# Eight stationary operands of the weight matmuls moved to byte offsets that are no multiples of 32

## The chip, the cores and the metric

The kernel runs on one core of one Trainium2 chip. The metric is the device time of one execution in microseconds; less is better. Before the change, three runs took 1162.81, 1162.16 and 1159.4 us (median 1162.16 us). TensorE (PE in the profile) multiplies; its weight loads, which put the stationary operand into the array, have rows of their own (PEld). VectorE is DVE, ScalarE is ACT, GpSimd is POOL, and SP only issues DMAs.

## The reference, cut to what matters

One layer of a hybrid encoder on 256 tokens of width 2048:

```python
h = rms_norm(x, norm_g)
proj = h @ w_in                      # 2048 x 16512, split into 15 parts
ya = chunked_band_attention(...) * silu(az)
yb = rwkv7_time_mix(...) * silu(bz)
yc = memory_cross_attention(cq, mk, mv) * silu(cz)   # mk, mv from rms_norm(mem) @ w_mem_kv
merged = (sigmoid(ga) * (ya @ w_up_a) + sigmoid(gb) * (yb @ w_up_b)
          + sigmoid(gc) * (yc @ w_up_c))
return x + merged @ w_o
```

All tensors are float32. The weights (w_in, w_mem_kv, the three w_up and w_o) are read once each.

## The kernel before

**Matmuls with weights.** A float32 product is made of three matmuls in a faster float32 format (float32r): both sides are split into a high and a low part, and high*high, low*high and high*low are summed in PSUM. The weights come as one stream: a DMA on the SP queue brings 128 x 2048 numbers (1 MB) into a buffer `raw` (two buffers), and `wchunk` makes of each two halves `whi` (ACT, line 191) and `wlo` (DVE, line 193), in four buffers each. `proj` (lines 197 to 218) runs, for every 128 rows of the weights and each of the two halves of the tokens, the matmuls of lines 210, 211 and 215: the weights (`whi`, `wlo`) are the moving operand, 512 columns wide, and a 128 x 128 block of the activations is the stationary one:

```python
T.matmul(acc[tt], xh[:, kt + k2, sl], hv[:, k2], start=(kt + k2 == 0), stop=False)
T.matmul(acc[tt], xl[:, kt + k2, sl], hv[:, k2], start=False, stop=False)
```

So each of these matmuls has a weight load of its own, of 128 numbers (512 bytes) per partition. `proj_last` (lines 220 to 249) does the same for the last quarter of w_o, partly with 256 columns. `proj_cm` (lines 251 to 265) has the roles turned: a weight block is stationary, `xh` and `xl` move with 256 columns.

**The activations.** Each is held as a pair of tiles, high and low, of 128 partitions by k times 256 numbers. `xh`, `xl` hold the normalised x (k = 16) and are used all along. `mh`, `ml` (k = 16) hold the memory, and are written by `split_kt` (lines 309, 310) in the first 27 us. `ych`, `ycl` hold the cross-attention's output, `yah`, `yal` the band attention's; both pairs use the same two slots `yth`, `ytl` (k = 8) and are written by `split_y` (lines 373, 374). `yh`, `yl` (k = 8) hold the output of the time mixing, and `gh`, `gl` (k = 16) the merged result; `to_T` writes them (lines 389, 390).

**Where the tiles stand.** SBUF is a byte range per partition. The pools hand out places one after the other, from the left or (side="right") from the right, each tile rounded up to 32 bytes. Tiles that nothing uses (`padw`, 24 numbers; `padr`, 56 numbers) shift what stands behind them. By the built program's own addresses, every operand of lines 210 to 262 begins at a multiple of 64 bytes before the change. `padr` is the rightmost tile, then come `ytl`, `yth`, and left of them the right-hand pools that follow each other in time: `mkv` with `catt`, later `rwkv`.

**Order.** Instructions of an engine run in the order of the program. Small generators (`spawn`, `tick`, `finish`) weave the attention's and the time mixing's steps between the weight chunks. The change touches none of this.

Of the kernel before, what the change touches and what calls it, by code (L numbers as in the profile page):

```python
# [9 lines left out]
F32R = mybir.dt.float32r  # L10
# [7 lines left out]
S = 256  # L18
P = 128
# [71 lines left out]
def build(nc, tc, A, out, dbg=None):  # L91
    dbg = dbg or {}
    ctx = ExitStack()
    with ctx:
        _build(ctx, nc, tc, A, out, dbg)


def _build(ctx, nc, tc, A, out, dbg):
    uid = [0]

    def nm(s):
        uid[0] += 1
        return f"{s}_{uid[0]}"

    def pool(st, name, bufs=1, side=None, space=None):
        kw = {}
        if side:
            kw["side"] = side
        if space is not None:
            kw["space"] = space  # L110
        return st.enter_context(tc.tile_pool(name=name, bufs=bufs, **kw))

    V, SC, G, T = nc.vector, nc.scalar, nc.gpsimd, nc.tensor

    cp = pool(ctx, "const")
    wp = pool(ctx, "wts")
# [5 lines left out]
    def t(pl, shape, tag, dtype=F32, bufs=1):  # L122
        return pl.tile(shape, dtype, name=nm(tag), tag=tag, bufs=bufs)
# [19 lines left out]
    def spawn(gen, wait=0):  # L143
        tasks.append([wait, gen])
        tick(0)
        return gen
# [13 lines left out]
    def finish(gen):  # L160
        for tk in list(tasks):
            if tk[1] is gen:
                while tk in tasks:
                    advance(tk)
# [5 lines left out]
    def wload():  # L170
        i = wstate[0]
        wstate[0] += 1
        raw = t(wp, [P, 2048], "raw", bufs=2)
        if i == 0:
            for a, b in ((0, 512), (512, 1024), (1024, 2048)):
                nc.sync.dma_start(raw[:, a:b], A["wstream"][i][:, a:b])
                yield raw
        else:
            nc.sync.dma_start(raw, A["wstream"][i])
        while True:  # L180
            yield raw
# [198 lines left out]
    def to_T(src, yh, yl, k0, k1):  # L380
        for k in range(k0, k1, 4):
            banks = [psum([P, 2, S]) for _ in range(2)]
            for kk in range(4):
                for tt in range(2):
                    T.transpose(banks[kk // 2][:, kk % 2, tt * P:tt * P + P],
                                src[:, tt, (k + kk) * P:(k + kk + 1) * P], ident)
            for i, bank in enumerate(banks):
                ks = slice(k + 2 * i, k + 2 * i + 2)
                SC.copy(yh[:, ks, :], bank)
                V.tensor_tensor(out=yl[:, ks, :], in0=bank, in1=yh[:, ks, :].bitcast(F32), op=ALU.subtract)  # L390
            yield 1
# [5 lines left out]
    xl = t(xpool, [P, 16, S], "xl", F32R)  # L397

    padp = pool(ctx, "padr", side="right")
    t(padp, [P, 56], "padr")  # L400
    yc_st = ExitStack()
    ycp = pool(yc_st, "yc", side="right")
    ych = t(ycp, [P, 8, S], "yth", F32R)
    ycl = t(ycp, [P, 8, S], "ytl", F32R)

    cst_ = ExitStack()
    mkp = pool(cst_, "mkv", side="right")
# [1 line left out]
    mv = t(mkp, [P, 2, 1024], "mv")  # L409
    m_st = ExitStack()  # L410
    mp = pool(m_st, "memT")
    mh = t(mp, [P, 16, S], "mh", F32R)
    ml = t(mp, [P, 16, S], "ml", F32R)
    wld = wload()
    raw0 = next(wld)
    xr0 = t(mp, [P, 4, S], "xraw", bufs=2)
# [522 lines left out]
    dump("merged_c", merged)  # L939


    yah = t(ycp, [P, 8, S], "yth", F32R)
    yal = t(ycp, [P, 8, S], "ytl", F32R)
    at_st = ExitStack()
    ap_ = pool(at_st, "aatt")

# [96 lines left out]
    dump("y_b", zb)  # L1043
    g_st = ExitStack()
    gp = pool(g_st, "gb")
    yh = t(gp, [P, 8, S], "yh", F32R)
    yl = t(gp, [P, 8, S], "yl", F32R)
    yt = spawn(to_T(zb, yh, yl, 0, 8), 1)
    sigs.append(gate_sig(proj(xh, xl, 16), zbp, 8))
    finish(yt)  # L1050
    gh = t(gp, [P, 16, S], "gh", F32R)
    gl = t(gp, [P, 16, S], "gl", F32R)
    for j in range(4):
        up(yh, yl, j, False, sigs[j])
        mt = spawn(to_T(merged, gh, gl, j * 4, j * 4 + 4), 1)
# [79 lines left out]
```

## Time and profile before

| what | value |
|---|---|
| runs, median (lowest, highest) | 1162.16 us (1159.4, 1162.81) |
| the profiled execution | 1159.04 us |
| its span, first to last instruction | 1157.0 us |
| PE busy | 1141.6 us, 6650 records |
| PE weight loads busy | 966.9 us |
| DVE, ACT, POOL busy | 791.2, 521.9, 178.3 us |
| mean granted TensorE clock | 0.997 |

A PE record's length is not its cost, since matmuls overlap in the array: the cost is the distance from one start to the next. A float32r matmul has one record, a plain float32 one has two. The chain of waits follows the work that ended last back from the end; its pieces show how long a row of equal matmuls took.

### The profile page before, as it was taken

Reading aid. Unit: us, or ns where it says so; the run is one execution under the profiler, and the core shown is the slowest. Engines: PE = TensorE matmul, PEld = TensorE weight load, DVE = VectorE, ACT = ScalarE, POOL = GpSimd, SP = SyncE. Lnnn points to the kernel's source line nnn. Section 1 sums busy time; section 2 is a strip of 40 time slices with the busy share of each in tenths; the row PEclk is TensorE's granted clock in tenths of the full one; section 3 lists DMA queues with packets and bytes.
Section 4 is the critical chain, followed back from the end, with each engine's and each line's share of the span. In section 5 each row is a group of like instructions: output and inputs, shape, how many; then the busy total and the mean of one; then the engine's idle time right before and its main releaser. Section 6 shows DMA issues by size and latency. Waiting matters only on the chain.

```text
span 1157.0 us, 16950 instructions
## 1 busy us (share of the span) xinstructions
PE 1141.6 (99%) x6650; PEld 966.9 (84%) x6650; DVE 791.2 (68%) x1370; ACT 521.9 (45%) x647; POOL 178.3 (15%) x240
## 2 busy tenths in 40 slices
PE   8999999999999999999999989999999999999998
PEld 6888989889889778988997869887888877888887
DVE  6974556557769667879866678946687856557443
ACT  7754545443643434344633526442453343444431
POOL 0110000034110204010203310203301203300000
PEclk9999999999999999999999989999999999999999
DMA  8756535466464653565644445564355664654663
GB/s 272 263 205 204 191 134 182 155 201 209 163 234 150 205 188 142 186 210 164 201 147 146 139 164 176 165 206 148 127 205 183 201 218 146 203 195 156 234 231 109
DMA packets 36906, 212.75 MB, mean 184 GB/s; under 512 B 5087, under 2 KB 7391, under 8 KB 13275
## 3 DMA queue, kind: packets, MB, share of 16 engines
q1 hardware_dynamic: 29664, 198.59, 50.0%
q0 software_dynamic: 3936, 9.44, 3.1%
q10 hardware_dynamic: 3226, 3.65, 1.0%
q8 instruction: 52, 0.85, 0.3%
q14 instruction: 28, 0.22, 0.1%
HBM read 206.95 MB, written 3.67 MB: 182 GB/s over the span
## 4 chain that ended last, share of the span: by engine, by line
PE 82%; DVE 8%; DMA 5%; ACT 2%; issue 1%; POOL 1%; SPq 0%; ACTq 0%; DVEq 0%; POOLq 0%
PE pp L210 21%; PE pp L211 20%; PE pp L215 19%; PE pp L259 4%; PE pp L260 4%; DMA raw<-in_wstream_dram 4%; PE pp L262 4%; DVE wlo L193 3%; ACT whi L191 1%; DVE Xu L751 1%; DVE tmu L749 1%; PE pp L232 1%; PE pp L234 1%; PE pp L231 1%; PE ps L496 1%
## 5 line engine op out<-in xcount | busy, mean ns | idle before, releaser
L193 DVE TENSOR_TENSOR wlo<-raw,whi 128x1024 fp32r<-128x1024 f32 x368 | 455.3, 1247 | 264.2 <-ACT whi L191 258.1
L191 ACT CAST whi<-raw 128x1024 fp32r<-128x1024 f32 x368 | 381.5, 1051 | 559.6 <-PE pp L211 274.8
L210 PE MATMUL pp<-whi,xh 128*128 128x512 f32 x768 | 308.1, 401 | 0.7 <-ACT whi L191 0.6
L211 PE MATMUL pp<-whi,xl 128*128 128x512 f32 x768 | 300.5, 391 | 0.0
L215 PE MATMUL pp<-wlo,xh 128*128 128x512 f32 x768 | 205.9, 390 | 2.3 <-DVE wlo L193 2.3
L210 PEld LDWEIGHTS pp<-whi,xh 128*128 128x128 f32 x768 | 144.7, 188 | 33.5 <-ACT whi L191 1.2
L215 PEld LDWEIGHTS pp<-wlo,xh 128*128 128x128 f32 x768 | 144.3, 188 | 33.5 <-DVE wlo L193 3.2
L211 PEld LDWEIGHTS pp<-whi,xl 128*128 128x128 f32 x768 | 144.9, 189 | 28.3
L259 PE MATMUL pp<-xh,whi 128*128 128x256 f32 x528 | 131.7, 287 | 0.0
L260 PE MATMUL pp<-xl,whi 128*128 128x256 f32 x528 | 129.3, 283 | 0.0
L259 PEld LDWEIGHTS pp<-xh,whi 128*128 128x128 f32 x528 | 101.0, 191 | 1.1 <-issue 0.3
L260 PEld LDWEIGHTS pp<-xl,whi 128*128 128x128 f32 x528 | 101.1, 192 | 0.4
L262 PE MATMUL pp<-xh,wlo 128*128 128x256 f32 x528 | 74.1, 283 | 0.0
L262 PEld LDWEIGHTS pp<-xh,wlo 128*128 128x128 f32 x528 | 68.1, 192 | 0.0
L210 PE MATMUL pp<-whi,mh 128*128 128x512 f32 x128 | 51.5, 402 | 2.7 <-ACT whi L191 2.3
L210 PE MATMUL pp<-whi,yth 128*128 128x512 f32 x128 | 51.1, 399 | 0.0
L211 PE MATMUL pp<-whi,ml 128*128 128x512 f32 x128 | 50.5, 394 | 0.0
L211 PE MATMUL pp<-whi,ytl 128*128 128x512 f32 x128 | 49.9, 390 | 0.0
L749 DVE TENSOR_TENSOR tmu<-Tu,Xu 128x112 f32<-128x112 f32 (+29 forms) x124 | 32.7, 263 | 9.5 <-DMA Tu<-scrt 6.3
L210 PE MATMUL pp<-whi,gh 128*128 128x512 f32 x96 | 37.4, 390 | 0.0
L211 PE MATMUL pp<-whi,gl 128*128 128x512 f32 x96 | 37.4, 389 | 0.0
L879 POOL TENSOR_TENSOR s0z<-st,fx 64x128 f32<-64x128 f32 x24 | 11.0, 458 | 168.2 <-DVE st L873 124.9
(258 smaller groups left out, 1367.1 us busy)
## 6 DMA issues: line engine op xcount, KB each, us to landing
raw<-in_wstream_dram SPq DMA_DIRECT2D x184, 1024.0 KB, 4.9
xraw<-in_xT_dram SPq DMA_DIRECT2D x8, 256.0 KB, 4.5
Tu<-scrt POOLq DMA_DIRECT2D x4, 512.0 KB, 4.1
xr<-in_x_dram POOLq DMA_DIRECT2D x8, 256.0 KB, 4.6
xraw<-in_memT_dram SPq DMA_DIRECT2D x7, 256.0 KB, 4.8
out_dram<-xr POOLq DMA_DIRECT2D x6, 256.0 KB, 3.8
bias<-in_rel_dram POOLq DMA_DIRECT2D x4, 256.0 KB, 4.1
tmpA<-in_bc_dram ACTq DMA_DIRECT2D x8, 128.0 KB, 4.1
```

Source lines behind the costliest of these rows:

```text
L191: SC.copy(hi, sl)
L193: V.tensor_tensor(out=lo, in0=sl, in1=hi.bitcast(F32), op=ALU.subtract)
L210: T.matmul(acc[tt], xh[:, kt + k2, sl], hv[:, k2], start=(kt + k2 == 0), stop=False)
L211: T.matmul(acc[tt], xl[:, kt + k2, sl], hv[:, k2], start=False, stop=False)
L215: T.matmul(acc[tt], xh[:, kt + k2, sl], lv[:, k2], start=False, stop=(last and k2 == 1))
L231: T.matmul(acc, xh[:, kt + k2, sl], hv[:, k2, cs], start=(kt + k2 == 0), stop=False)
L232: T.matmul(acc, xl[:, kt + k2, sl], hv[:, k2, cs], start=False, stop=False)
L234: T.matmul(acc, xh[:, kt + k2, sl], lv[:, k2, cs], start=False, stop=(kt + k2 == nk - 1))
L259: T.matmul(acc, hv[:, k2], xh[:, kt + k2, :], start=(kt + k2 == 0), stop=False)
L260: T.matmul(acc, hv[:, k2], xl[:, kt + k2, :], start=False, stop=False)
L262: T.matmul(acc, lv[:, k2], xh[:, kt + k2, :], start=False, stop=(kt + k2 == 15))
L749: V.tensor_tensor(out=tv, in0=Tu[:, s, s + 1:32].unsqueeze(2).to_broadcast([P, n, m]), in1=X[:, s:s + 1, 0:m].to_broadcast([P, n, m]), op= ...
```

## The change

`toff` makes a tile that is 8 numbers (32 bytes) per partition larger and returns a slice of it that begins `off` numbers in. The eight tiles are made by it, the offsets being 2, 4 or 6 numbers, so 8, 16 or 24 bytes. `padr` shrinks from 56 to 48 numbers, and a new unused tile `pady` (56 numbers) stands at the head of the pool of `yh`, `yl`, `gh`, `gl`.

```diff
+    def toff(pl, k, tag, off):
+        v = t(pl, [P, k * S + 8], tag, F32R)
+        return v[:, off:off + k * S].rearrange("p (k s) -> p k s", s=S)
...
-    t(padp, [P, 56], "padr")
+    t(padp, [P, 48], "padr")
...
-    ych = t(ycp, [P, 8, S], "yth", F32R)
-    ycl = t(ycp, [P, 8, S], "ytl", F32R)
+    ych = toff(ycp, 8, "yth", 2)
+    ycl = toff(ycp, 8, "ytl", 2)
...
-    mh = t(mp, [P, 16, S], "mh", F32R)
-    ml = t(mp, [P, 16, S], "ml", F32R)
+    mh = toff(mp, 16, "mh", 4)
+    ml = toff(mp, 16, "ml", 4)
...
-    yah = t(ycp, [P, 8, S], "yth", F32R)
-    yal = t(ycp, [P, 8, S], "ytl", F32R)
+    yah = toff(ycp, 8, "yth", 2)
+    yal = toff(ycp, 8, "ytl", 2)
...
-    yh = t(gp, [P, 8, S], "yh", F32R)
-    yl = t(gp, [P, 8, S], "yl", F32R)
+    t(gp, [P, 56], "pady")
+    yh = toff(gp, 8, "yh", 4)
+    yl = toff(gp, 8, "yl", 6)
...
-    gh = t(gp, [P, 16, S], "gh", F32R)
-    gl = t(gp, [P, 16, S], "gl", F32R)
+    gh = toff(gp, 16, "gh", 6)
+    gl = toff(gp, 16, "gl", 4)
```

The places that follow, in bytes within a partition, by the addresses of the two built programs:

| operand | begins before | begins after | rest by 32 | rest by 64 |
|---|---|---|---|---|
| yth | 212736 | 212712 | 8 | 40 |
| ytl | 220928 | 220936 | 8 | 8 |
| mh | 92160 | 92176 | 16 | 16 |
| ml | 108544 | 108592 | 16 | 48 |
| yh | 150528 | 150768 | 16 | 48 |
| yl | 158720 | 159000 | 24 | 24 |
| gh | 166912 | 167224 | 24 | 56 |
| gl | 183296 | 183632 | 16 | 16 |

Every block that a weight load reads lies a multiple of 512 bytes behind its tile's begin, so it has the same rests. `xh`, `xl`, `raw`, `whi` and `wlo` stay where they are, at multiples of 64. All tiles of the pools `mkv`, `catt` and `rwkv` move 32 bytes to the left, as their pools end where `yth` begins, so a rest of 0 by 64 becomes 32 and the other way round; `xr` goes from rest 0 to 32. The number and the order of instructions are the same on every engine.

## Rows read from the trace of the kernel before

**Rows 1.** The page: engines' busy time, and the chain by line.

```profile
PE 1141.6 (99%) x6650; PEld 966.9 (84%) x6650; DVE 791.2 (68%) x1370; ACT 521.9 (45%) x647; POOL 178.3 (15%) x240
PE pp L210 21%; PE pp L211 20%; PE pp L215 19%; PE pp L259 4%; PE pp L260 4%; DMA raw<-in_wstream_dram 4%; PE pp L262 4%; DVE wlo L193 3%; ACT whi L191 1%; DVE Xu L751 1%; DVE tmu L749 1%; PE pp L232 1%; PE pp L234 1%; PE pp L231 1%; PE ps L496 1%
```

**Rows 2.** Timeline of PE in an up-projection: start us, length us, instruction.

```profile
304.87 0.39 PE L210 MATMUL pp<-whi,yth 128*128 128x512 f32 x1
305.10 0.39 PE L211 MATMUL pp<-whi,ytl 128*128 128x512 f32 x1
305.33 0.39 PE L210 MATMUL pp<-whi,yth 128*128 128x512 f32 x1
...
306.69 1.07 PE L215 MATMUL pp<-wlo,yth 128*128 128x512 f32 x4
```

**Rows 3.** The chain of waits: start us, us, what, and how many.

```profile
24.07 0.91 PE pp L215 x4
125.37 0.96 PE pp L262 x8
147.35 3.46 PE ps L496 x16
```

**Rows 4.** Timeline of PE, the program's first matmuls with weights.

```profile
6.92 0.63 PE L211 MATMUL pp<-whi,ml 128*128 128x512 f32 x1
7.35 0.63 PE L210 MATMUL pp<-whi,mh 128*128 128x512 f32 x1
7.78 0.63 PE L211 MATMUL pp<-whi,ml 128*128 128x512 f32 x1
8.20 0.63 PE L210 MATMUL pp<-whi,mh 128*128 128x512 f32 x1
```

**Rows 5.** Timeline of the weight loads, just after a wait for whi.

```profile
15.92 0.19 PEld L210 LDWEIGHTS pp<-whi,mh 128*128 128x128 f32 x1 [2.40 <-ACT whi L191]
16.02 0.19 PEld L211 LDWEIGHTS pp<-whi,ml 128*128 128x128 f32 x1
```

**Rows 6.** Groups of PE by shape: xcount, then busy us and mean ns of one.

```profile
L210 PE MATMUL pp<-whi,mh 128*128 128x512 f32 x128 | 51.5, 402 | 2.7 <-ACT whi L191 2.3 <-ACT whi L454 0.4
L210 PE MATMUL pp<-whi,yth 128*128 128x512 f32 x128 | 51.1, 399 | 0.0
L210 PE MATMUL pp<-whi,gh 128*128 128x512 f32 x96 | 37.4, 390 | 0.0
L210 PE MATMUL pp<-whi,yh 128*128 128x512 f32 x64 | 25.2, 393 | 0.0
L231 PE MATMUL pp<-whi,gh 128*128 128x256 f32 x32 | 8.3, 282 | 0.0
L231 PE MATMUL pp<-whi,gh 128*128 128x512 f32 x16 | 6.3, 392 | 0.0
```

**Rows 7.** Busy us of each engine by stretch, then granted clock, DMA share, GB/s.

```profile
core 0: us, PE busy (x) PEld busy (x) DVE busy (x) ACT busy (x) POOL busy (x), PEclk, DMA share, GB/s
0.00:25.00 25.00, 19.58 (x93) 15.67 (x94) 15.46 (x27) 16.92 (x28) 2.09 (x10) 1.00 0.80 267
25.00:105.00 80.00, 80.00 (x366) 66.45 (x366) 59.81 (x88) 50.02 (x66) 8.66 (x11) 1.00 0.68 230
297.00:395.00 98.00, 97.44 (x546) 83.94 (x545) 76.89 (x167) 37.85 (x40) 12.44 (x18) 1.00 0.58 191
990.00:1070.00 80.00, 80.00 (x379) 66.78 (x378) 51.39 (x56) 37.26 (x43) 8.10 (x10) 1.00 0.55 186
1070.00:1113.00 43.00, 43.00 (x192) 35.59 (x191) 21.74 (x21) 16.87 (x16) 3.26 (x6) 1.00 0.68 230
```

**Rows 8.** Weight loads of two plain float32 lines: duration ns min/median/max.

```profile
L808 PEld LDWEIGHTS ps<-D,av x128: 101/108/108, 400.7 to 934.7; 32*32 32x32 f32 x128
L817 PEld LDWEIGHTS ps<-D1T,M x128: 101/108/108, 409.7 to 943.8; 32*32 32x32 f32 x128
```

**Rows 9.** Four lines of DVE: duration ns min/median/max.

```profile
L297 DVE TENSOR_TENSOR xraw<-xraw x6: 420/423/425, 15.7 to 72.4; 128x256 f32<-128x256 f32 x6
L602 DVE TENSOR_TENSOR rk<-rkraw x16: 411/420/1518, 265.2 to 607.1; 128x256 f32<-128x256 f32 x16
L600 DVE TENSOR_TENSOR rkraw<-pp,rstdbc x16: 411/426/427, 263.8 to 606.1; 128x256 f32<-128x256 f32 x16
L366 DVE TENSOR_TENSOR qn<-pp,rstdbc x16: 404/418/425, 142.0 to 724.9; 128x256 f32<-128x256 f32 x16
```

## The prediction, as it was made

> **What bounds the kernel now.** I read the page first. PE is busy 99% of the span, and some two thirds of the chain that ended last are the matmuls of lines 210 to 215, with lines 259 to 262 behind them; DMA and DVE hold single per cents [rows 1]. A busy PE is no proof, since its records overlap, so I read the stretches next. Where the eight operands are used PE has hardly a hole: 80.0 of 80 us in 25 to 105 and in 990 to 1070, 43.0 of 43 us in 1070 to 1113. Only at the start (19.6 of 25 us) and, by less, in 297 to 395 does it wait for chunks of weights [rows 7]. So a cost or a gain per matmul reaches the end of the kernel almost one for one.
>
> Then I read what one matmul costs, from starts: 304.87, 305.10, 305.33, so 0.227 us for 512 columns [rows 2]. The chain says it more finely. Four matmuls of 512 columns take 0.91 us, 227 ns each; eight of 256 columns take 0.96 us, 120 ns each [rows 3]. The difference, 107 ns for 256 columns, is one column per cycle at 2.4 GHz. So 512 columns are 213.3 ns, and 13.3 ns are left over for each matmul, at either width. What is it? Plain float32 matmuls of 256 columns (line 496, two records each, 16 records in 3.46 us) take 216 ns for what is 213.3 ns at two cycles per column: 2.7 ns left over, and each has a weight load of the same 512 bytes [rows 3]. The first matmuls of the program follow each other by 0.43 us, which is 512 columns at 1.2 GHz (426.7 ns) with next to nothing left over [rows 4]; that this was the lower clock I read from the distance alone. So the remainder shows only where the moving stream runs at its full rate. That fits two readers in each other's way, the moving stream and the load of the next stationary block, and it is the one place where the begin of a stationary operand can matter.
>
> **The change part by part.** No instruction is added, removed or moved; only addresses differ. There are four things to cost.
>
> (1) *Matmuls whose stationary operand has moved.* Line 210 has 128 with mh, 128 with yth, 64 with yh and 96 with gh; line 231 has 32 and 16 with gh [rows 6]. Lines 211 and 215, and 232 and 234, have as many each, so 3 x (128 + 128 + 64 + 96 + 48) = 1392 matmuls. The load itself is hidden: two loads behind a wait start 0.10 us apart [rows 5], so a load needs about 0.1 us of the 0.227 us that a matmul of 512 columns lasts. Only 96 matmuls, those of 256 columns in the last projection, have little room (0.120 us). What is not hidden is the remainder of 13.3 ns. No matmul of this trace has an operand off a multiple of 32 bytes, so I bound it from both sides: the remainder may vanish (-13.3 ns) or double (+13.3 ns, if a load that straddles reads everything twice). Times 1392 that is -18.5 to +18.5 us. Between these ends: 13.3 ns for 512 bytes is 0.83 ns for each 32 bytes, and a load that begins within such a piece touches 17 pieces for 16, so +0.83 ns, +1.2 us in all. The nearest row with a shifted stationary operand is line 808 against line 817: of av, which stands 32 bytes off a multiple of 64, and of M1, which stands on one. Their loads take 108 ns both [rows 8]. It is near in kind and far in load on the reader, since these are plain float32 matmuls, which have no remainder. I take +0.6 us, half way between nothing and one piece more.
>
> The Trainium skill has a rule that makes the step coarser (SBUF — State Buffer, "Specifications (TRN2)"): lines of 16 bytes, at least two hits of a line needed for the full rate. No row here shows a line. By it offsets of 16 bytes cost nothing, those of 8 and 24 touch 33 lines for 32 and still have two hits on the first and last, and the sum would be an estimated 0.3 us in place of 0.6.
>
> (2) *What writes and re-reads these operands.* By the code, 36 ACT and 36 DVE instructions: 16 each for the memory, 8 for the two attentions, 12 for yh and gh. Now they write at shifted addresses, and DVE reads the high part there. The nearest rows are on DVE: line 602 reads one input 4 bytes off, median 420 ns, against 423 ns for line 297 with both inputs in place; line 600 writes 4 bytes off, 426 ns, against 418 ns for line 366 [rows 9]. So between -3 and +8 ns an instruction, under 0.3 us for 36 in a row on one engine, and beside PE's work but for the first chunks. I take 0. If ACT were slower where DVE is not, the cover is the weight chunks in stock; without it the first 16 blocks of mh would pay, some 16 times the excess.
>
> (3) *Tiles that only move by multiples of 32 bytes* (the pools of the cross-attention and the time mixing, xr). Rows 8 stand for them on PE; before the change such tiles stand at both rests, and line 808's loads are no slower. I take 0. The bound: the right-hand tiles' instructions lie between weight chunks, under PE's stream.
>
> (4) *pady and padr* are never touched: 0.
>
> The sum: 1159.0 (profiled, span 1157.0) + 0.6 = 1159.6 us. The profiled execution lies 3.1 us under the median of the runs, 1162.2 us, and the new time is again a median of runs, so I forecast 1162.8 us. The forecast's own range is the runs' lowest, 1159.4, to the highest with the whole piece and a rest for the runs, 1166 us.
>
> **The rivals.** *Slower: every piece of the load straddles.* If the load fetches pieces of a fixed size from where the operand begins, and these cross a boundary each, each piece costs two reads, and the remainder goes from 13.3 to 26.7 ns. Place: all 1392 matmuls. For it: the remainder is there only at the full rate of the moving stream, as with a reader that is full [rows 3, 4]. Against: the loads of line 808 show nothing of a shift [rows 8], and DVE streams run over a shifted begin for nothing [rows 9]. Price: 18.5 us, less what is hidden where PE waits anyway: 61 of the matmuls lie before 25 us and 96 in 297 to 395, 157 x 13.3 ns = 2.1 us at most. So 1162.2 + 17 = 1179 us. It decides from 2.5 ns a matmul, where 1392 of them make 3.5 us.
>
> *Faster: the two readers no longer meet.* Before, both the moving and the stationary operands begin at multiples of 64, so the same pieces may be asked for in step; at 8, 16 or 24 bytes they aren't. The remainder would fall to that of line 496, 2.7 ns, and save 10.6 ns x 1392 = 14.8 us, some 13 us after what is hidden, so 1149 us; a part of it gives a part. For it: rows 3 and 4 as above. Against: the two streams run at different speeds, a load of 512 bytes beside 2048 bytes of the moving operand, so they pass through every relation to each other whatever their begin, and three different offsets would all have to help.
>
> Two statements of the Trainium skill bear on both (TensorE: Matmul & The Clock Gate, "Part 2: What happens when you issue a matmul" and "Back-to-back issue gap"): the load has a read port of its own and takes nothing from the moving stream, and the gap over N / 2.4 is 2.5 ns. The trace agrees for line 496 (2.7 ns) and not for the float32r lines (13.3 ns). By that page neither rival could be and the time would stay; by the rows they can.
>
> *Nothing that the change says.* The slices could have ended at the old rests; by the built program's addresses they have not, so this has no chance of its own.
>
> **How the numbers follow.** 0.3%, 3.5 us, is about what a measurement of this kernel can tell from no change. The forecast, no change that can be told, gets 0.57: the nearest rows show no cost of a shift, and the one row that could speak for either rival, the remainder, needs a particular mechanism for each. Slower gets 0.22 (doubling 0.15, a lesser part over 2.5 ns, or ACT and the moved tiles, 0.07). Faster gets 0.21 (the whole remainder 0.09, a part of it 0.12). The range reaches to 1150 us, which takes in most of a gain by parts and leaves the whole one out, and to 1180 us, which takes in the doubling.
>
> **What would show it.** In the changed kernel's chain, four matmuls of line 219 (215 before) with mh, yth, yh or gh should take 0.91 us as those with xh do, and the starts of lines 214 and 215 with yth should be 0.227 us apart. 0.96 us for four would be the doubling, 0.87 us the gain. Line 313's and 394's medians (309, 390) should stay within 10 ns. Whatever moves in matmuls with xh, or in plain float32 ones, is no part of (1). A time outside 1159 to 1166 us with distances of 227 ns unchanged would mean that a wait for weights grew or shrank, which none of these steps has.

## The result and the profile after

The changed kernel takes 1165.86 us (median of 9 runs, 1163.9 to 1170.02), the kernel before beside it 1160.26 us (9 runs, 1157.74 to 1162.81). The ratio is 1.0051, with a 95% interval of 1.0038 to 1.0064: 5.9 us slower. The forecast was 1162.8 us and no change that can be told. The time lies inside the range given (1150 to 1180 us), but the interval leaves out 1, and the sign is that of the slower case.

The page of the changed kernel, busy time and the chain by line (lines are 4 further on: 210, 211, 215 are now 214, 215, 219; 259, 260, 262 are 263, 264, 266):

```profile
PE 1148.3 (99%) x6650; PEld 968.4 (83%) x6650; DVE 791.7 (68%) x1370; ACT 523.5 (45%) x647; POOL 178.4 (15%) x240
PE pp L214 23%; PE pp L219 22%; PE pp L215 22%; PE pp L263 5%; PE pp L264 5%; PE pp L266 5%; DVE wlo L197 2%; PE ps L717 1%; PE pp L235 1%; PE pp L238 1%; PE pp L236 1%; PE ps L535 1%; PE ps L500 1%; PE ps L841 1%; PE ps L848 1%
```

Against [rows 1], PE is busy 6.7 us longer with the same 6650 records, and the span grew by 6.8 us (1157.0 to 1163.8). DVE, ACT and POOL stand within 1.6 us. So PE does not wait longer; its matmuls take longer. Which ones? The timeline of PE in the up-projection of [rows 2] (start us, length us, instruction), where a stretch with `xh` turns into one with `yth`:

```profile
305.21 0.39 PE L214 MATMUL pp<-whi,xh 128*128 128x512 f32 x1
305.44 0.39 PE L215 MATMUL pp<-whi,xl 128*128 128x512 f32 x1
305.67 0.39 PE L214 MATMUL pp<-whi,xh 128*128 128x512 f32 x1
...
307.02 1.08 PE L219 MATMUL pp<-wlo,xh 128*128 128x512 f32 x4
307.94 0.40 PE L214 MATMUL pp<-whi,yth 128*128 128x512 f32 x1
308.18 0.39 PE L215 MATMUL pp<-whi,ytl 128*128 128x512 f32 x1
308.40 0.40 PE L214 MATMUL pp<-whi,yth 128*128 128x512 f32 x1
...
309.79 1.09 PE L219 MATMUL pp<-wlo,yth 128*128 128x512 f32 x4
```

With `xh` eight matmuls take 307.02 - 305.21 = 1.81 us, 226 ns each, as before. With `yth` they take 309.79 - 307.94 = 1.85 us, 231 ns each, where [rows 2] have 306.69 - 304.87 = 1.82 us, 227.5 ns. The chain of waits shows the same in groups of four (start us, us, what):

```profile
36.47 0.94 PE pp L219 x4
...
1005.44 0.91 PE pp L219 x4
...
1075.75 0.94 PE pp L219 x4
```

The first is in the memory's projections (`mh`), the second is one with `xh`, the third is in the stretch of `gh`: 0.94 us where the operand has moved, 0.91 us where it has not. [rows 3] have 0.91 us.

One finer measure serves all comparisons below: the mean distance from one matmul's start to the next over all matmuls of a kind in the trace, those after which PE waited left out (over 245 ns at 512 columns, over 140 ns at 256). In ns, with the count of matmuls:

| stationary operand (columns) | count | before | after | us in all |
|---|---|---|---|---|
| mh, ml (512) | 384 | 227.3 | 232.7 | +2.1 |
| yth, ytl (512) | 384 | 227.5 | 231.6 | +1.6 |
| yh, yl (512) | 192 | 226.9 | 229.5 | +0.5 |
| gh, gl (512) | 336 | 227.2 | 232.0 | +1.6 |
| gh, gl (256) | 95 | 119.4 | 117.9 | -0.1 |
| xh, xl (512) | 2304 | 227.6 | 227.6 | 0 |
| weights, lines 259 to 262 (256) | 1584 | 119.9 | 119.9 | 0 |

Below, m, yt, y, g and x stand for the pairs `mh` and `ml`, `yth` and `ytl`, `yh` and `yl`, `gh` and `gl`, `xh` and `xl`, each with its matmuls of 512 columns.

The sum is +5.6 us, beside 5.9 us by the ratio. The profiled spans are 6.8 us apart, and the clock is enough for what is left: by the granted clock the execution after ran some 10 us at half clock (1.2 GHz), near 18, 680 and 725 us, the one before some 7 us, near 690 us. That is an estimated 1.7 us more lost, if PE had work all the while. The last of the three, by stretch (us; PE busy, granted clock, DMA share, GB/s), of the changed kernel:

```profile
716.00:724.00 8.00, 5.60 (x41) 1.00 0.53 195
724.00:727.00 3.00, 3.00 (x16) 0.51 0.36 153
727.00:738.00 11.00, 11.00 (x56) 0.98 0.29 100
```

PE had been idle for 2.4 of 8 us, and then ran for 3 us at half clock, which is 1.5 us lost. In the profile of before the same place, 722 to 728 us, shows a granted clock of 1.00.

The steps that were taken at nothing: the writers on ACT and DVE, and the plain float32 loads of [rows 8] (lines 808 and 817 then, 812 and 821 now), as the trace after has them (duration ns, min/median/max).

```profile
L313 ACT ACTIVATE mh<-xraw,vec x16: 489/497/513, 5.1 to 24.7; 128x256 fp32r<-128x256 f32 x16
...
L812 PEld LDWEIGHTS ps<-D,av x128: 101/108/108, 403.4 to 939.6; 32*32 32x32 f32 x128
...
L821 PEld LDWEIGHTS ps<-D1T,M x128: 101/108/108, 412.6 to 948.6; 32*32 32x32 f32 x128
```

Line 313 writes `mh` with a median of 497 ns where the trace before has 496. The two loads keep their 108 ns.

### The profile page after: what moved, and what is told of

It reads as the page before. It is cut to its first block, busy times and chain, and to the rows that moved or that the text cites. A ratio compares the mean times of both kernels' runs of the same rounds, so it can differ in the third digit from the quotient of the medians.

```text
span 1163.8 us, 16950 instructions
## 1 busy us (share of the span) xinstructions
PE 1148.3 (99%) x6650; PEld 968.4 (83%) x6650; DVE 791.7 (68%) x1370; ACT 523.5 (45%) x647; POOL 178.4 (15%) x240
## 4 chain that ended last, share of the span: by engine, by line
PE 91%; DVE 5%; DMA 2%; POOL 1%; ACT 1%; issue 1%; SPq 0%; DVEq 0%; POOLq 0%; ACTq 0%
PE pp L214 23%; PE pp L219 22%; PE pp L215 22%; PE pp L263 5%; PE pp L264 5%; PE pp L266 5%; DVE wlo L197 2%; PE ps L717 1%; PE pp L235 1%; PE pp L238 1%; PE pp L236 1%; PE ps L535 1%; PE ps L500 1%; PE ps L841 1%; PE ps L848 1%
```

## The experiments

One reading of the addresses was too coarse ahead of the change. Before it, the operands of all matmuls with weights begin not only at multiples of 64 bytes but at multiples of 256. After it, by 256, `mh` begins at 16, `ml` 48, `yth` 232, `ytl` 8, `yh` 240, `yl` 24, `gh` 56, `gl` 80, while the moving weights still begin at 0. All begins below are by 256, which is what is left of the address over a multiple of 256 bytes. The trace before shows that one need count no further: there `yth` and `ytl` begin 256 bytes off a multiple of 512 and all other operands on one, and yt stands at 227.5 ns, the rest at 226.9 to 227.6. Ahead of the change only the rests of the eight operands by 32 and 64 were looked at. The larger tiles also put the places of `ml`, `yth`, `yh`, `gh` and `gl` 32 or 64 bytes away from where they stood. Where a time below has no ratio beside it, it is that of one execution; what such a run shows is its distances, each a mean over some 190 matmuls or more.

**Offsets of zero.** Is it the begin off 32 bytes, or the neighbours that moved by 32? The changed kernel with all eight offsets 0 keeps pads and larger tiles; `mh` begins at 0, `ml` 32, `yth` 224, `ytl` 0, `yh` 224, `yl` 0, `gh` 32, `gl` 64.

```diff
-    mh = toff(mp, 16, "mh", 4)
+    mh = toff(mp, 16, "mh", 0)
```

(and so for the other seven)

> The changed kernel with all eight offsets at 0: the larger tiles, padr and pady stay, so all neighbours stand where the change put them, and the eight operands begin at multiples of 32 (ml, yth, yh and gh at 32 by 64). Theory A (the begin of the stationary operand by 32 bytes costs each matmul some ns): distances of 512 columns return from 229 to 236 ns to 227 ns and the ratio to the kernel before is 0.998 to 1.002. Theory B (the loss comes from the tiles that only moved by 32 bytes): distances of the eight stay at 229 to 236 or the waits stay longer, ratio 1.003 to 1.007. Theory C (the rest by 64 counts): the matmuls with ml, yth, yh and gh stay above 227 ns, those with mh, ytl, yl and gl return, ratio about 1.0025.

Measured: ratio 1.0054 (1.0039 to 1.0068), 1164.96 us. The groups m, yt, y and g stand at 232.6, 233.0, 233.1 and 231.6 ns. Its timeline, first of eight and the row behind the eighth:

```profile
42.13 0.40 PE L214 MATMUL pp<-whi,mh 128*128 128x512 f32 x1
...
44.00 1.08 PE L219 MATMUL pp<-wlo,mh 128*128 128x512 f32 x4
```

1.87 / 8 = 234 ns. The whole loss is there with no operand off a multiple of 32, so it does not take the straddling of 32 bytes that the prediction argued about. (That a begin off 32 costs nothing is not shown by this; the run with both at 8, the last one below, shows otherwise.) But the loss sits in the same matmuls, so it is not the neighbours either (their lines stand as before). `mh` itself is at 0 here, as before the change: that its matmuls alternate with those of `ml`, at 32, is enough, and even two matmuls with `mh` behind each other start 229.9 ns apart.

**Two scans of the offset.** Tiles 16 numbers larger on places that are multiples of 64; m, yt, y, g read 8, 16, 24, 4 bytes further on in the first, 16, 24, 4, 8 in the second.

```diff
-    mh = t(mp, [P, 16, S], "mh", F32R)
+    mh = toff(mp, 16, "mh", 2)        # scan 1; 4 in scan 2
```

> The kernel before with tiles 16 numbers larger, all at multiples of 64, and the two operands of a pair at one offset: mh, ml 8 bytes; yth, ytl 16; yh, yl 24; gh, gl 4 (an odd number of elements). Theory A: distances above 227 ns in all four pairs, by 0.8 ns if one piece more is read, by 4 to 8 ns as in the changed kernel; time 1164 to 1168 us. If a boundary of 16 bytes were what counts, yth and ytl (16) would be at 227 ns and the other three above. Theory B: 227 ns everywhere and 1160 us.

> As the run before it, with the offsets passed on: mh, ml 16 bytes; yth, ytl 24; yh, yl 4; gh, gl 8. If the offset sets the distance, 16 bytes gives mh here what it gives yth there, 8 gives gh here what it gives mh there, 24 gives yth what it gives yh, 4 gives yh what it gives gh, each within 1 ns. If the stage sets it, the stages keep their distances: time 1164 to 1168 us in both cases.

Measured: 1168.63 and 1166.4 us, one execution each. The groups m, yt, y, g stand at 231.7, 232.9, 231.4, 233.7 ns in the first and at 232.1, 230.4, 232.4, 232.8 ns in the second. Offset by offset (4 bytes: 233.7 and 232.4; 8: 231.7 and 232.8; 16: 232.9 and 232.1; 24: 231.4 and 230.4) there is no order in it. The scans didn't separate anything: high and low tiles here also stood at different multiples of 64, and the next runs show that these count.

**Only the moving operand.** The activations stay at 0; the `whi`, `wlo` tiles get 8 numbers more and are read 16 bytes further on, so they begin at 16, 48, 80, up to 240.

```diff
-            hi = t(wp, [P, 1024], "whi", F32R, bufs=4)
+            hi = t(wp, [P, 1032], "whi", F32R, bufs=4)[:, 4:4+1024]
```

> The kernel before with the weights' tiles whi and wlo begun 16 bytes off a multiple of 32, and all activations at multiples of 64: in lines 210 to 215 the moving operand is shifted and the stationary one is not, in lines 259 to 262 the other way round. If the shift of the stationary operand alone counts: 227 ns for 512 columns, and another distance than 120 ns for 256 columns in lines 259 to 262 (the changed kernel has 116 to 118 there for shifted gh and gl, so about 1584 x 3 ns = 5 us less). If the distance between the two begins counts: 229 to 236 ns for some 3700 matmuls of 512 columns, 15 to 25 us more, 1175 to 1185 us. If neither, 1160 us.

Measured: 1170.69 us, span 1168.6. All 512-column groups stand at 231.7 to 232.1 ns, `xh` too (231.8); lines 259 to 262 fall to 118.6. So it takes no move of the stationary operand: either side will do. The expectation by distance had the 512 columns right (229 to 236 ns) and the time too long (1175 to 1185 us).

**Offsets by 64.** If alignment to 64 were enough, this costs nothing. m is read at 64, `yth` at 128 and `ytl` at 128, y at 192; g has larger tiles too but begins at 0.

```diff
-    mh = t(mp, [P, 16, S], "mh", F32R)
+    mh = toff(mp, 16, "mh", 16)
...
-    yh = t(gp, [P, 8, S], "yh", F32R)
+    yh = toff(gp, 8, "yh", 48)
...
-    gh = t(gp, [P, 16, S], "gh", F32R)
+    gh = toff(gp, 16, "gh", 0)
```

> Slices of larger tiles again, but at 64 bytes (mh, ml), 128 (yth, ytl), 192 (yh, yl) and 0 (gh, gl), counted from a multiple of 256. Theory C (64 bytes count: an operand must begin at a multiple of 64): 227 ns in all four pairs and a ratio to the kernel before of 0.998 to 1.002. If the boundary is larger (128 or 256), the pairs at 64 and 192, or all but gh and gl, stay at 229 to 236 ns, ratio 1.002 to 1.004. If the larger tile itself is what costs (theory P), all four pairs stay above 227 ns, ratio 1.004 to 1.007.

Measured: ratio 1.0033 (1.0017 to 1.0049), 1163.4 us; m 233.3 ns, yt 232.5, y 229.1, g 227.2. Eight matmuls with `mh`, and eight with `gh`:

```profile
42.77 0.40 PE L214 MATMUL pp<-whi,mh 128*128 128x512 f32 x1
...
44.64 1.10 PE L219 MATMUL pp<-wlo,mh 128*128 128x512 f32 x4
```

```profile
1080.57 0.39 PE L214 MATMUL pp<-whi,gh 128*128 128x512 f32 x1
...
1082.38 1.07 PE L219 MATMUL pp<-wlo,gh 128*128 128x512 f32 x4
```

1.87 / 8 = 234 ns, and 1.81 / 8 = 226 ns. A begin at 64 or at 128 is slow, one at 192 less so, and a larger tile that begins at 0 is not slow.

**All at 32.** Weights, x, m, y and g begin at 32, by two pads; only `yth`, `ytl` stand at 224.

```diff
-    t(cp, [P, 24], "padw")
+    t(cp, [P, 32], "padw")
-    t(padp, [P, 56], "padr")
+    t(padp, [P, 64], "padr")
```

> The kernel before with padw and padr each 32 bytes larger, so that weights and activations alike begin 32 bytes off a multiple of 64, moving and stationary, everywhere. If only the distance between the two begins counts (theory R): 227 and 120 ns as before, 1160 us. If each must begin at a multiple of 64 (theory C): 229 to 236 ns in lines 210 to 215 with every operand, about 3700 matmuls x 5 ns = 18 us more, 1175 to 1180 us.

Measured: 1161.55 us, span 1159.5. x, m, y and g stand at 227.7, 227.5, 226.9 and 227.2 ns, as before to 0.2 ns; yt at 229.2. Eight with `mh` and eight with `yth`:

```profile
41.45 0.39 PE L210 MATMUL pp<-whi,mh 128*128 128x512 f32 x1
...
43.26 1.07 PE L215 MATMUL pp<-wlo,mh 128*128 128x512 f32 x4
...
306.02 0.39 PE L210 MATMUL pp<-whi,yth 128*128 128x512 f32 x1
...
307.86 1.08 PE L215 MATMUL pp<-wlo,yth 128*128 128x512 f32 x4
```

1.81 / 8 = 226 ns and 1.84 / 8 = 230 ns. Moving both sides by the same 32 bytes costs nothing. What counts is the distance between the two begins: stationary minus moving, by 256. For yt it is 224 - 32 = 192, and y at 192 in the run before stood at the same 229 ns.

**Moving at 32, the rest elsewhere.** Weights at 32, x, m, y, g at 64 (distance 32), yt at 0 (distance 224).

```diff
+    sm.tile([P, 8], F32, name="pads", tag="pads", bufs=1)
...
-    t(cp, [P, 24], "padw")
+    t(cp, [P, 32], "padw")
```

> The kernel before with raw, whi and wlo 32 bytes off a multiple of 64 and all activations at multiples of 64: only the moving operand of lines 210 to 215 (and the stationary one of 259 to 262) is off. Theories R and C both: 229 to 236 ns in lines 210 to 215, 1168 to 1180 us. If only the stationary operand's begin counts: 227 ns in lines 210 to 215, and 115 to 122 ns in lines 259 to 262.

Measured: 1176.87 us, span 1174.8: every 512-column group at 233.1 to 233.2 ns, 3600 x 5.65 = 20.3 us more, while lines 259 to 262 fall from 119.9 to 116.7 ns, 4.9 us less. That is 15.4 us by the groups, 17.8 by the spans. All operands begin at multiples of 32 here.

**Only x.** Tiles of `xh`, `xl` 8 numbers larger, read 8 bytes further on, and `padw` cut, so that `xh` begins at 200, `xl` at 232, the weights at 192, and the other activations stay at 0 (distance 64).

```diff
-    xh = t(xpool, [P, 16, S], "xh", F32R)
+    xh = toff(xpool, 16, "xh", 2)
...
-    t(cp, [P, 24], "padw")
+    t(cp, [P, 8], "padw")
```

> The dose: the kernel before with only xh and xl moved, to 8 and 40 bytes by 64; the eight operands stay at multiples of 64. They are the stationary operand of 2304 matmuls of 512 columns (1392 in the change) and the moving one of 1584 of 256 columns. If the cost is per matmul: 229 to 236 ns with xh and xl alone, 2304 x 4.8 ns = 11 us more than before, less what is hidden in stretches that wait for weights, 1168 to 1172 us; 227 ns with mh, yth, yh, gh.

Measured: 1171.73 us, span 1169.7. The time is the one expected, but not for the reason given, since the shorter `padw` moved the weights too. x, a mixture of distances 8 and 40, stands at 230.7 ns; the four untouched groups, to which the weights now stand at another distance, at 233.2 to 233.4, as m in the run of the offsets by 64, also at distance 64. In the last projection the sign is the other way. Timeline of its 256-column matmuls here, and of the kernel before:

```profile
1146.11 0.28 PE L235 MATMUL pp<-whi,gh 128*128 128x256 f32 x1
...
1146.56 0.39 PE L238 MATMUL pp<-wlo,gh 128*128 128x256 f32 x2
```

```profile
1132.24 0.28 PE L231 MATMUL pp<-whi,gh 128*128 128x256 f32 x1
...
1132.72 0.40 PE L234 MATMUL pp<-wlo,gh 128*128 128x256 f32 x2
```

Four take 0.45 us at distance 64 and 0.48 us at distance 0: 113 and 120 ns. So at this distance 256 columns gain about what 512 columns lose. Lines 259 to 262, at distances 248 and 216 here, stay at 119.4. That points to a version faster than both kernels: lines 259 to 262 have 256 columns and are 1584.

**Weights 64, 128 or 8 bytes further on in `proj_cm` alone.** All 512-column work stays at distance 0. Two scratch tiles share a place with others to make room.

```diff
-        for hi, lo in wchunk():              # in proj_cm
+        for hi, lo in wchunk(16):            # 32 and 2 in the other two
...
-            hi = t(wp, [P, 1024], "whi", F32R, bufs=4)
+            hi = t(wp, [P, 1088], "whi", F32R, bufs=4)[:, off:off + 1024]
...
-        tm = t(rp, [P, 192], "tmu")
+        tm = t(rp, [P, 256], "D1T")
-        Xt = t(rp, [P, 8, 32], "tmx")
+        Xt = t(rp, [P, 8, 32], "M1")
```

> Before with one change: in the projections of L259 to L262 (proj_cm, 1584 matmuls of 256 columns), where the weights are the stationary operand, the four whi and four wlo tiles are read 64 bytes further on (tiles 256 bytes longer, slice from element 16), while the activations stay at 0 by 256 bytes; every 512-column projection keeps begins at 0 on both sides. To make room two small scratch tiles (tmu, tmx) take the places of D1T and M1. The theory that only the distance between the begins counts (stationary minus moving, by 256 bytes): at 64 the 256-column matmuls of the last projection took 113 ns in the run with the x operands at 200 and the weights at 192, against 119.4 at 0, so these 1584 go from 119.9 to 113 ns, 1584 x 6.5 = 10 us less, about 1150 us, ratio 0.991; the 512-column matmuls stay at 227. The rival, that the 113 ns belonged to a moving operand that itself begins at 192, or to that place in the program: cm stays at 117 to 120 ns and the time at 1156 to 1160, ratio 0.997 to 1.000. The theory that any slice off a multiple of 256 costs: slower, 1584 x 3 = 5 us.

> As the run at 64, with the weights of proj_cm read 128 bytes further on. The distance theory has no row for 256 columns at 128; by the 512-column row at 128 (232.5 ns, nearly the 233.3 of 64) it expects nearly the gain of 64: 113 to 114 ns, 1584 x 6 = 9.5 us less, ratio 0.992. By the rival there is none (117 to 120 ns).

> As the run with the weights of proj_cm 64 bytes further on (ratio 0.9967), with 8 bytes in place of 64, so that the begins in proj_cm are neither equal by 256 bytes nor multiples of 32, and all 512-column projections stay at 0. In the run with weights, m, y and g all at 8 the same 1584 matmuls stood at 115.8 ns. If a row goes over from that program to this one: 115.8 ns against 119.85 of before, 1584 x 4.05 = 6.4 us less, ratio 0.9945, and every call of proj_cm near 115.5, not split into calls at 113 and calls at 118 as the run at 64 was. If a begin off a multiple of 32 costs by itself whatever the column count: no gain or a loss, 120 ns or more.

Measured: at 64, ratio 0.9967 (0.9954 to 0.9979), 1155.2 us, the 1584 matmuls at 116.4 ns; at 8, ratio 0.9965 (0.9951 to 0.9979), 1156.22 us, 115.8 ns; at 128, ratio 1.0006 (0.9995 to 1.0016), 119.3 ns. The 512-column groups stay at 226.9 to 227.6 ns in all three. So two of the three beat the kernel before, by 0.3%, but by less than expected, and the gain expected at 128 did not come. That run has the same two scratch tiles moved, so their move is not what gains. At 64 the expectation of 113 ns was met in some rows of matmuls and not in others; a row is what `proj_cm` issues without other matmuls between, 24 to 192 of them. The chain of waits of that kernel, eight matmuls at two places ([rows 3] have 0.96 us):

```profile
125.91 0.94 PE pp L262 x8
...
453.94 0.91 PE pp L262 x8
```

That is 117.5 and 113.8 ns. A whole row runs at the one or at the other: all seven rows before 371 us at 118, and of the 20 later ones 14 at 113, five at 118 and one at half clock, all with the same begins by 256. In the run at 8 there is one level, about 115.5 ns, at both places (0.92 us for eight):

```profile
127.20 0.92 PE pp L262 x8
...
457.60 0.92 PE pp L262 x8
```

And by the groups 1584 x 3.5 = 5.5 us should have come at 64, where spans give 1157.0 - 1153.1 = 3.9. The profile has 3 us at half clock in these lines that the kernel before has not at that place:

```profile
716.00:719.00 3.00, 3.00 (x16) 0.50 0.41 175
```

But by the granted clock both executions lost 3.4 us to half clock in all, this one near 687 and 717 us, the one before near 690, so the clock does not explain the rest. Where it went is not shown.

**Both at 8.** A last test of the distance: weights, m, y and g begin at 8, x and yt at 0.

```diff
-    mh = t(mp, [P, 16, S], "mh", F32R)
+    mh = toff(mp, 16, "mh", 2)
...
-            hi = t(wp, [P, 1024], "whi", F32R, bufs=4)
+            hi = t(wp, [P, 1088], "whi", F32R, bufs=4)[:, 2:1026]
```

> Before with the weights (whi, wlo) and the operands m, y and g all begun 8 bytes behind a multiple of 256, none at a multiple of 32; x and yt stay at 0. Distance theory: m, y and g at 226.9 to 227.5 ns as before (distance 0), though both operands straddle every 32 bytes; x and yt at a distance of 248 are slower, 229 to 233 ns, so 2688 x 4 = 10 us more in all, about 1170 us. The rival that a begin off 32 bytes costs by itself (on either side): m, y and g at 230 to 233 ns as well.

Measured: 1173.09 us, span 1171.0. m, y and g stand at 231.2, 231.3 and 230.9 ns, not at 227. Eight with `mh`:

```profile
42.35 0.39 PE L214 MATMUL pp<-whi,mh 128*128 128x512 f32 x1
...
44.20 1.08 PE L219 MATMUL pp<-wlo,mh 128*128 128x512 f32 x4
```

1.85 / 8 = 231 ns. x and yt (distance 248) stand at 233.2. So the distance alone is not the whole rule: here begins off a multiple of 32, on both sides, cost 4 ns at distance 0. Which of the two sides costs it was not tried. The two conditions together give 227 ns: equal begins by 256, and these at a multiple of 32 (seen at 0 and at 32).

## Why the prediction was right or wrong

The groups of 512 columns in which high and low operands had one begin each, so that a single distance held throughout (the other groups, those of the changed kernel among them, mix several and stand at 229.5 to 233.7 ns):

| stationary, moving begin | distance | ns a matmul | from |
|---|---|---|---|
| 0, 0 and 32, 32 | 0 | 226.9 to 227.7 | before; all at 32 |
| 8, 8 | 0 | 231 | both at 8 |
| 64, 32 | 32 | 233.2 | moving at 32 |
| 64, 0 and 0, 192 | 64 | 233.3 | offsets by 64; only x |
| 128, 0 | 128 | 232.5 | offsets by 64 |
| 192, 0 and 224, 32 | 192 | 229.1, 229.2 | offsets by 64; all at 32 |
| 0, 32 | 224 | 233.2 | moving at 32 |
| 0, 8 | 248 | 233.2 | both at 8 |

**What bounds the kernel** was right: PE has no hole there, and a cost per matmul reached the end almost one for one (5.6 us by the groups, 5.9 by the ratio). Lines 210 to 215 hold 60% of the chain [rows 1], a little less than the two thirds that it read.

**The time.** That 1165.86 us lies even within the narrower range, 1159.4 to 1166 us, is luck. The forecast stood on a median of three runs, 1162.16 us, where nine give 1160.26; this made up for 1.9 of the 5.0 us by which the sum was too small by the groups. By its size, what came is the slower rival's lesser part, which had 0.07 together with ACT and the moved tiles.

**Step 1, the size of the term,** failed. 0.6 us were taken and 5.6 us came, 4.0 ns for each of 1392 matmuls, above the 2.5 ns from which the slower case decided and well inside the bound of 13.3. It was sized by one more piece of 32 bytes in a load; the run with offsets of zero has no such piece more and loses the same. So it looked at the rest of a begin by 32 alone, and put the part of a move that is a whole number of 32 bytes at nothing. `ml`, `yth`, `yh`, `gh` and `gl` move by such amounts alone in the run with offsets of zero, and the 4.4 to 6.1 ns a matmul of their groups are all of its loss. The remainder of 13.3 ns was the right place to look: it grows to about 20 ns (233.3 - 213.3).

**Step 1, the mechanism.** The slower rival, every piece of the load straddling, is not needed for the loss (offsets of zero), and its 0.96 us for four matmuls didn't come (0.94). It is not refuted either: with both begins at 8, distance 0, a matmul takes 231 ns. So two things are each enough for a loss, unequal begins and begins off 32, and the changed kernel has both. The faster rival had the right ingredient, that the relation of the two streams' begins matters, and the wrong sign: the kernel before already stood at the best of the relations tried for 512 columns. The argument against it, that the streams "pass through every relation to each other whatever their begin", is refuted by the table. Why the same relation is the best for 512 columns and not for 256, and by what mechanism the two streams hinder each other, no run shows.

**Step 3, tiles that only move by multiples of 32 bytes taken at 0,** held for the tiles that it names. The loads of [rows 8] kept their 108 ns, and line 500 (496 before), where `mkT` and `cqT` both went from 0 to 224, takes in the chain of after what it took in [rows 3] (3.46 us):

```profile
150.45 3.45 PE ps L500 x16
```

What failed is the same thought carried over to the eight operands, in step 1. These are plain float32 lines, which have next to no remainder; the prediction named that difference and used the rows all the same. Its look at the addresses stopped at 64 bytes, where before and after differ by 256.

**Steps 2 and 4 and the clause on x** were right: lines 313 and 394 moved by at most 1 ns, matmuls with `xh` and lines 259 to 262 by 0.1 ns at most.

**Two pages of the Trainium skill.** By the Trainium skill (TensorE: Matmul & The Clock Gate, "Part 2: What happens when you issue a matmul" and "Back-to-back issue gap") the load has its own read port and the gap over N / 2.4 is 2.5 ns, in the second of these sections for a matmul by itself. The trace does not agree for a row of float32r matmuls with a load each: their gap is 13.3 ns or up to 20 ns by where the two operands begin. By the Trainium skill's lines of 16 bytes (SBUF — State Buffer, "Specifications (TRN2)") the run with offsets of zero should have lost nothing; it lost 0.54%.

**Still open:** whether a begin off 32 bytes adds anything once the begins differ (after, with offsets, lost 5.9 us, and 6.3 us without); which side's begin off 32 costs; whether 16 bytes would do in place of 32; and what decides between the two levels, 113 and 118 ns, of a row at distance 64.

## What to carry to other kernels

When an operand becomes a slice of a larger tile, compare its begin with that of the operand it meets, by 256 bytes: for float32r matmuls of 512 columns in an unbroken row the two were fastest when equal and at multiples of 32 (0 and 32 were tried), and alignment to 32, 64 or 128 alone did not keep that pace. For 256 columns equal begins were not the best: 8 or 64 bytes apart saved 0.3% of this kernel, and 128 apart nothing. A remainder in the distance from start to start, over columns by clock, is the place where this shows, and lines without one say nothing about it.

## What the runs showed of the hardware

Beside the relation of the begins: a row of 256-column matmuls at distance 64 keeps one of two paces, 113 or 118 ns, for its whole length, up to 192 matmuls, though the begins by 256 are the same. The five rows that began 226 ns behind a 512-column matmul all ran at 118, and the one that began 236 ns behind one ran at 113; those behind small plain float32 matmuls went either way, and the pace was there within some six matmuls. The run at 128 splits too: all six rows that began behind a 512-column matmul ran at 120 ns, and 19 of the other 21 at 118.3 to 118.8. Its chain of waits has one row of either kind:

```profile
126.83 0.96 PE pp L262 x8
...
456.67 0.95 PE pp L262 x8
```

That points to how a row is entered, which no run changed on purpose; a mean over a program can mix the two.
